# Attention pairs that take values, keys and queries in another order, with the value products moved into the score tiles

## The chip, the cores and the metric

The kernel runs on one core of one Trainium2 chip. The metric is the device time of one execution in microseconds (us); of several runs the median counts. A profile is one execution recorded by the hardware profiler. TensorE multiplies and transposes into PSUM; VectorE, ScalarE and GpSimd (DVE, ACT and POOL in the profile) work on what lies there and in SBUF; SyncE (SP) issues the transfers.

## What is computed

The reference is a block of two layers over 1024 latent and 256 context tokens of width 1024. Each layer norms its input, projects it, runs three mixers side by side (a gated linear recurrence with 4 heads, an mLSTM with 4 heads, and windowed attention with 6 heads of 64), gates their outputs, projects them back and adds the normed result to the input. The change lies in the attention:

```
def row_fn(r):                       # one of 16 rows of 64 latent tokens
    s_w = q_r . k(8 rows around r) + bias        # 16 columns around each query, else -inf
    s_c = q_r . k(context)                       # 256 keys, no bias
    p = softmax(concat(s_w, s_c))
    return p_w @ v(8 rows) + p_c @ v(context)
```

In layer 0 the 256 context tokens attend to one another too, without bias. In layer 1 only the latent tokens have outputs.

## The kernel before

All projections read the normed input, transposed, as a high and a low half, so each product is three matmuls (`mm`, line 311, through `cm_group`, line 344; transposes go through `tr`, line 317). A projection unit is one generator that yields after every three matmuls of one k of eight: a group of 512 tokens gives 8 yields; with the 256 context tokens a unit has 8 + 8 + 8 yields (the first 8 half as long), without them 16. `c0` to `c2` are the keys of the three head pairs (`natten_k`, line 1047), `d0` to `d2` the queries (`natten_q`, line 1074), `e0` to `e2` the values (`natten_v`, line 1059), `G0` to `G7` gates of the mixers' outputs (`gate_unit`, line 405; G2 to G4 have two projections). `W` loads the output weights (`out_weights`, line 1244: 32 loads, each rounded by ScalarE at line 1264 and subtracted by GpSimd at line 1265, into the buffers of the normed input), and `o0` to `o9` are tiles of the output projection (`out_tile`, line 1310; matmuls named u).

The order of TensorE's work is written by a planner, `drive` (line 455). It runs one generator, `mixers` (line 1413), whose own matmuls (recurrences, attention) go first; each number that this yields is a time in the planner's clock (`clk`, which every matmul advances by its columns / 2400, half of that for small ones) that is to be filled. It is filled by steps of units from `ORDER` (line 44), one unit at a time and each to its end; the next one is the first in the list whose conditions in `NEED` (line 53) are met. Yielding a name runs units until that one is done. If nothing can run, the clock is set forward and TensorE simply waits for its next operand. The waits are in `WAIT` (line 54). The other engines are put in order by a scheduler that sees the whole program; `ahead` gives instructions a priority.

After the two pairs of recurrence heads (`hgrn_head`, line 898; VectorE runs its state chain at line 989, the last products into op are at line 1011) the condition `o1` is set, the second recurrence norm follows (`hgrn_norm`, line 1016), and the attention pairs 0, 1 and 2 come. Before each, `mixers` asks for `c`, `d` and `e` of the pair, then transposes and splits the values (`natten_vt`, line 1094). `natten_pair` (line 1116) works in blocks of 128 queries and two heads: 2 + 8 blocks in layer 0, 8 in layer 1. A block has these parts:

- `scores` (line 1136): one PSUM tile of two banks (pool pb, two buffers, tiles sc) per head. Window scores end at column 512, the 256 context scores follow. The bias tile (tag RB, two buffers) gets the window bias by DMA and zeros for the context by a GpSimd memset (line 1143). VectorE adds both and takes the row's minimum (line 1156), ScalarE takes the exponential (1158) and divides (1160).
- `context` and `window` (lines 1169 and 1177): the probabilities are transposed in tiles tc and tw of pool pm (two buffers) and split by ScalarE and VectorE (lines 1166 and 1167) into Pc and Pw.
- `values` (line 1186): products of 10 matmuls in a tile pv of pool pm, emptied by ScalarE (1198) and VectorE (1199 and twice 1215).

The blocks are staggered, and the waits lie between:

```
b.context(); b.window(0); yield WAIT["t"]     # 0.3
nxt.scores()
b.window(1); yield WAIT["pt"]                 # 1.2
b.values();  yield WAIT["sc"]                 # 1.2, 3.0 after the first scores
```

So each block takes four buffers of pool pm in turn: tc, tw, tw, pv. Buffers `wt(i, ...)` are shared slots of SBUF. The values of a pair lie in slots 10 and 3, in which the blocks keep their split probabilities (Pw in 10 and 9, Pc in 3); the keys lie in slots (4, 5) and (0, 8) by turns; the queries of all pairs in 6 and 7. Therefore `e1` and `e2` wait for the end of the pair before (`n0`, `n1`), `d1` and `d2` for its last scores (`s0`, `s1`), while `c1` and `c2` can fill the blocks of the pair before.

Of the kernel before, what the change touches and what calls it, by code (L numbers as in the profile page):

```python
# [21 lines left out]
KD = 8  # L22
# [21 lines left out]
ORDER = ("p0 p1 v q0 p2 f0 f1 p3 q1 f2 f3 G0 G1 c0 G2 d0 e0 G3 c1 G4 d1 e1 c2 G5 d2 e2 G6 G7 W",) * 2  # L44
# [8 lines left out]
NEED = {"p2": ("b0",), "p3": ("b1",), "c0": ("A0",), "d0": ("o1",), "e0": ("A1",), "c1": ("o1",), "G4": ("o1",), "d1": ("s0",), "e1": ("n0",), "c2": ("s0",), "d2": ("s1",), "e2": ("n1",), "W": ("c2", "d2", "e2", "G7", "gg")} | {f"o{t}": ("W",) for t in range(10)}  # L53
# [10 lines left out]
def _build(ctx, tc, nc, I, out, dbg, upto):  # L64
# [40 lines left out]
    XS = ((3, 4, 5, 6, 8, 1, 11, 7, 9, 3), (1, 2, 3, 9, 11, 12, 6, 7, 4, 5))  # L105
# [10 lines left out]
    V.memset(mhalf, -0.5)  # L116

# [929 lines left out]
    def natten_k(l, p, hx):  # L1047

        kh, kl = [wt(((4, 5), (0, 8))[p % 2][i], [P, TA], f"ck{l}_{p}_{i}", F32R) for i in range(2)]
# [9 lines left out]
    def natten_v(l, p, hx):  # L1059

        cv = S["cv", p] = [wt((10, 3)[i], [P, TC + 8 * CWID], f"cv{l}_{p}_{i}") for i in range(2)]
# [12 lines left out]
    def natten_q(l, p, hx):  # L1074
# [4 lines left out]
        def evq(t0, N, ps):  # L1079
# [9 lines left out]
            V.tensor_tensor(view(qs[1]), src, hi.bitcast(F32), op=ALU.subtract)  # L1089

        yield from proj_cm(hx, I["wcm"][l, 6 + 3 * p + 0], LATG if l == 1 else ALLG, evq, f"Cq{l}_{p}")
        S["q", p] = qs

    def natten_vt(l, p):
# [4 lines left out]
        for i, cbs in ((0, None), (0, (0, 3)), (0, (1, 2)), (1, (0, 3)), (1, (1, 2))):  # L1099
# [10 lines left out]
            for m in range(0, len(o), n):  # L1110
# [3 lines left out]
                V.tensor_tensor(lo, v, hi.bitcast(F32), op=ALU.subtract)  # L1114

    def natten_pair(l, p):
# [4 lines left out]
        if p == 2:  # L1121
            S["yC"] = wt(0, [P, TA], f"yC{l}")
# [3 lines left out]
        class Block:  # L1126
# [9 lines left out]
            def scores(self):  # L1136

                nm, nk, rb, cb = self.nm, self.nk, self.rb, self.cb
                self.S2, bias, ps = [], [], []
# [420 lines left out]
```

## Time and profile before

| | |
|---|---|
| median of three runs | 2108.16 us (2107.46 to 2115.57) |
| profiled execution | 2102.49 us, of it 2100.7 us span from first to last instruction |
| TensorE matmuls busy | 1816.6 us, 86% |
| VectorE / ScalarE / GpSimd busy | 1338.9 / 885.5 / 727.8 us |
| mean granted TensorE clock | 0.931 |
| transfers | 199.32 MB, a mean of 95 GB/s |

Times in rows are us from the first instruction. The attention of layer 0 lies between about 700 and 1080, that of layer 1 between about 1720 and 2025. In a timeline each row is a start, a length, the engine and line, the operation, what it writes and reads, and a count where equal neighbours are merged; in square brackets stands the idle time of the engine before it and what ended it. PEclk is the clock that TensorE was granted, as a share of 2.4 GHz; the lower level, 1.2 GHz, is 0.5.

### The profile page before, as it was taken

What the parts mean: (1) busy time and instruction counts of PE and PEld (TensorE: products, weight loads), DVE (VectorE), ACT (ScalarE), POOL (GpSimd) and SP (SyncE); (2) the same over time, 40 slices, a digit from 0 to 9 for tenths busy, and PEclk for the clock granted to TensorE, in tenths of its full rate; (3) what the DMA queues carried; (4) which work ended last, traced back from release to release, by engine and by line L of the source; (5) the groups of instructions that cost most, each with busy time, mean ns of one, the idle gap of its engine ahead of it and who ended that gap; (6) DMA issues with size and microseconds to landing.
All of it is one profiled execution on the core that took longest, in us unless ns stands there. A gap on an engine that the chain in (4) does not pass through costs nothing.

```text
span 2100.7 us, 34868 instructions
## 1 busy us (share of the span) xinstructions
PE 1816.6 (86%) x12842; PEld 1559.3 (74%) x12842; DVE 1338.9 (64%) x3117; ACT 885.5 (42%) x2029; POOL 727.8 (35%) x746
## 2 busy tenths in 40 slices
PE   6988889988878888987799988999979798988798
PEld 3977888877666776766678888989767677767577
DVE  7697777778498458353565586464786954443564
ACT  5433433453232256364553434353532325554641
POOL 5342342254371112024124444234454621201512
PEclk8989999998889999978899999999999999997799
DMA  7122333530311222134354112132404011213443
GB/s 301 61 80 74 106 111 108 171 108 26 114 39 44 91 83 96 34 99 143 99 190 142 35 45 84 50 124 97 147 32 131 26 53 50 87 35 94 141 137 106
DMA packets 143723, 199.32 MB, mean 95 GB/s; under 512 B 13128, under 2 KB 89960, under 8 KB 143552
## 3 DMA queue, kind: packets, MB, share of 16 engines
q1 hardware_dynamic: 143552, 197.09, 29.1%
q8 instruction: 101, 1.65, 0.3%
q14 instruction: 70, 0.57, 0.1%
HBM read 154.35 MB, written 42.70 MB: 94 GB/s over the span
## 4 chain that ended last, share of the span: by engine, by line
PE 45%; DVE 27%; issue 8%; ACT 8%; DMA 5%; POOL 4%; DVEq 0%; POOLq 0%; ACTq 0%; SPq 0%
PE u L315 8%; PE ppB L315 7%; DVE F L945 6%; PE ppCv L315 4%; PE ppCq L315 4%; PE ppAf L315 3%; DVE dj L199 3%; PE ppGz L315 3%; DVE S L989 2%; PE ppAq L315 2%; ACT S L1158 2%; PE ov L315 2%; PE ppAv L315 2%; ACT S L1160 2%; DVE AT L926 2%
## 5 line engine op out<-in xcount | busy, mean ns | idle before, releaser
L315 PE MATMUL ppB<-whB,hh 128*128 128x288 f32 (+3 forms) x640 | 198.2, 310 | 23.9 <-ACT Vx L606 18.3
L315 PE MATMUL ppB<-whB,hl 128*128 128x288 f32 (+3 forms) x640 | 193.2, 302 | 1.0 <-DVE hl L293 1.0
L315 PE MATMUL ppB<-wlB,hh 128*128 128x288 f32 (+3 forms) x640 | 193.1, 302 | 0.0
L315 PE MATMUL u<-ow,yh 128*128 128x512 f32 (+1 forms) x684 | 185.3, 365 | 0.3 <-ACT u L1386 0.3
L945 POOL TENSOR_TENSOR F<-F,FG 64x640 f32<-64x640 f32 x72 | 142.1, 1974 | 74.5 <-DVE FG L946 58.4
L945 DVE TENSOR_TENSOR F<-F,FG 64x640 f32<-64x640 f32 (+1 forms) x120 | 150.5, 1256 | 3.0
L199 DVE CUSTOM_DVE_ANT_0 dj<-wm,crows 128x256 bf16<-128x256 f32 x256 | 129.7, 507 | 32.3 <-DMA wm<-in_w_mod 28.9
L315 PE MATMUL ppGz<-hh,whGz 128*128 128x512 f32 (+1 forms) x320 | 132.5, 414 | 20.4 <-DVE gz L422 13.3
L315 PEld LDWEIGHTS ppB<-whB,hh 128*128 128x128 f32 x640 | 125.4, 196 | 26.8 <-ACT Vx L606 20.2
L315 PEld LDWEIGHTS u<-ow,yh 128*128 128x128 f32 x684 | 122.2, 191 | 19.2 <-ACT u L1386 0.5
L1143 POOL MEMSET bias<- 128x256 f32 x96 | 29.7, 312 | 297.5 <-DVE nmx L1156 283.4
L315 PEld LDWEIGHTS ppB<-whB,hl 128*128 128x128 f32 x640 | 125.0, 195 | 1.3 <-DVE hl L293 1.3
L315 PEld LDWEIGHTS ppB<-wlB,hh 128*128 128x128 f32 x640 | 125.3, 196 | 0.1
L315 PE MATMUL ppGz<-hh,wlGz 128*128 128x512 f32 (+1 forms) x320 | 123.8, 387 | 0.6 <-POOL wlGz L325 0.6
L315 PE MATMUL ppGz<-hl,whGz 128*128 128x512 f32 (+1 forms) x320 | 124.2, 388 | 0.0
L932 ACT ACTIVATE ZK<-F,half 128x640 f32<-128x640 f32 (+1 forms) x96 | 70.6, 786 | 106.0 <-POOL F L945 77.7
L315 PE MATMUL u<-ow,yl 128*128 128x512 f32 (+1 forms) x324 | 114.7, 372 | 0.0
L315 PE MATMUL gr<-F,ZK 128*64 128x64 f32 x1728 | 70.3, 245 | 48.4 <-DVE F L945 34.6
L315 PEld LDWEIGHTS gr<-F,ZK 128*64 128x64 f32 x1728 | 64.6, 158 | 59.3 <-issue 37.0
L315 PEld LDWEIGHTS ppGz<-hh,whGz 128*128 128x128 f32 x320 | 64.5, 201 | 34.8 <-DVE gz L422 15.3
L989 DVE SCALAR_TENSOR_TENSOR S<-S,dec,up 64x64 f32<-64x64 f32 x288 | 80.5, 280 | 9.2
L1158 ACT ACTIVATE S<-S,nmx 128x544 f32<-128x544 f32 (+1 forms) x96 | 75.1, 783 | 24.2 <-DVE nmx L1156 22.8
(443 smaller groups left out, 5327.8 us busy)
## 6 DMA issues: line engine op xcount, KB each, us to landing
wm<-in_w_mod SPq DMA_DIRECT2D x64, 256.0 KB
bias<-in_rpb SPq DMA_DIRECT2D x48, 192.0 KB
ygr<-gTd SPq DMA_DIRECT2D x36, 256.0 KB
wm<-in_w_first SPq DMA_DIRECT2D x16, 512.0 KB
wrGz<-in_wcm SPq DMA_DIRECT2D x32, 256.0 KB
gTd<-gz SPq DMA_DIRECT2D x32, 256.0 KB
wro<-in_w_out SPq DMA_DIRECT2D x32, 256.0 KB
wrB<-in_wB SPq DMA_DIRECT2D x24, 288.0 KB
```

The lines of the kernel that those rows point to most:

```text
L199: V.tensor_tensor_reduce(out=junk, in0=w, in1=r, scale=1.0, scalar=0.0, op0=ALU.mult, op1=ALU.add, accum_out=dst[:, i:i + 1])
L315: return PE.matmul(out, lhsT=lhsT, rhs=rhs, start=start, stop=stop)
L926: V.copy_predicated(AT[:, y0:, :], lmask[:, None, li, :].to_broadcast([P, NT - y0, LA]), src)
L932: A.activation(vw(ZK)[:, tok0 // (2 * m):, s_, :], vw(T1)[:, tok0 // (2 * m):, s_, :], AF.Copy, scale=half[:, s_:s_ + 1])
L945: eng.tensor_tensor(x, x, d[r, n0:].to_broadcast([64, nb - n0, m]), op=ALU.mult)
L989: V.scalar_tensor_tensor(Sx[r, nx, :], Sx[r, c, :], dec[r, c:c + 1], ups[c][r], op0=ALU.mult, op1=ALU.add)
L1143: G.memset(bias[i][:, nk:nk + TC], 0.0)
L1158: A.activation(S2, S2, AF.Exp, scale=-1.0, bias=nmx[:, o], accum_out=den[:, o])
L1160: A.activation(S2, S2, AF.Copy, scale=den[:, o])
```

## The change

The order in each pair becomes values, their transposes, keys, blocks. Values lie in slots 4 and 5; `e1` and `e2` need only the value transposes of the pair before (new conditions `vt0` and `vt1`); the keys always lie in 0 and 8 and wait for the last scores of the pair before, as do the queries. The first values (`e0`) take the place of the first keys among the units that run under the second pair of recurrence heads; `c0` waits for `o1`. `G7` waits for `s1`. A block waits for its own group of queries alone (context, first or second 512 tokens). The value products of a block go into columns 768 to 1023 of the two score tiles of the next block, in the bank of its context scores; only a pair's last block still takes a tile of pool pm. Their emptying is split by head. The context part of the bias comes as zeros with the bias DMA; blocks of context queries add a constant zero. Slots of the result of pair 2, of the low half in `out_prep` and of the next layer's input move with these.

```
-ORDER = ("... f3 G0 G1 c0 G2 d0 e0 G3 c1 G4 d1 e1 c2 G5 d2 e2 G6 G7 W",) * 2
+ORDER = ("... f3 G0 G1 e0 G2 c0 d0 G3 e1 G4 c1 d1 e2 G5 c2 d2 G6 G7 W",) * 2
...
-NEED = {..., "c0": ("A0",), "d0": ("o1",), "e0": ("A1",), "c1": ("o1",), "G4": ("o1",), "d1": ("s0",), "e1": ("n0",), "c2": ("s0",), "d2": ("s1",), "e2": ("n1",), "W": ("c2", "d2", "e2", "G7", "gg")}
+NEED = {..., "e0": ("A0",), "c0": ("o1",), "d0": ("o1",), "G4": ("o1",), "e1": ("vt0",), "c1": ("s0",), "d1": ("s0",), "e2": ("vt1",), "c2": ("s1",), "d2": ("s1",), "G7": ("s1",), "W": ("c2", "d2", "e2", "G7", "gg")}
...
-    XS = (..., (1, 2, 3, 9, 11, 12, 6, 7, 4, 5))
+    XS = (..., (0, 1, 2, 3, 9, 11, 12, 6, 7, 8))
...
+    zero = cst.tile([P, 1], F32, name="zero")
+    V.memset(zero, 0.0)
...
     def natten_k(l, p, hx):
-        kh, kl = [wt(((4, 5), (0, 8))[p % 2][i], [P, TA], f"ck{l}_{p}_{i}", F32R) for i in range(2)]
+        kh, kl = [wt((0, 8)[i], [P, TA], f"ck{l}_{p}_{i}", F32R) for i in range(2)]
...
     def natten_v(l, p, hx):
-        cv = S["cv", p] = [wt((10, 3)[i], [P, TC + 8 * CWID], f"cv{l}_{p}_{i}") for i in range(2)]
+        cv = S["cv", p] = [wt((4, 5)[i], [P, TC + 8 * CWID], f"cv{l}_{p}_{i}") for i in range(2)]
...
     def natten_q(l, p, hx):
...
             V.tensor_tensor(view(qs[1]), src, hi.bitcast(F32), op=ALU.subtract)
+            done.add(f"d{p}_{(t0 - TC) // 512 if t0 else None}")
+
+        S["q", p] = qs
         yield from proj_cm(hx, I["wcm"][l, 6 + 3 * p + 0], LATG if l == 1 else ALLG, evq, f"Cq{l}_{p}")
-        S["q", p] = qs
...
     def natten_vt(l, p):
...
+        done.add(f"vt{p}")
...
     def natten_pair(l, p):
...
-            S["yC"] = wt(0, [P, TA], f"yC{l}")
+            S["yC"] = wt(4, [P, TA], f"yC{l}")
...
             def scores(self):
...
-                    bias.append(sm.tile([P, NWIN + TC], F32, tag="RB", name=f"bias{nm}_{i}"))
-                    G.memset(bias[i][:, nk:nk + TC], 0.0)
+                    bias.append(sm.tile([P, NWIN + TC], F32, tag="RB", name=f"bias{nm}_{i}") if nk else None)
                     if nk:
-                        nc.sync.dma_start(bias[i][:, 0:nk], I["rpb"][l, 2 * p + i, 3 * rb + (0, 1, 1, 2)[cb], :, 0:nk])
+                        nc.sync.dma_start(bias[i][:, 0:nk + TC], I["rpb"][l, 2 * p + i, 3 * rb + (0, 1, 1, 2)[cb], :, 0:nk + TC])
...
-                    V.tensor_tensor_reduce(out=S2, in0=ps[i][:, 512 - nk:512 + TC], in1=bias[i][:, :nk + TC],
+                    V.tensor_tensor_reduce(out=S2, in0=ps[i][:, 512 - nk:512 + TC], in1=bias[i][:, :nk + TC] if nk else zero.to_broadcast([P, TC]),
...
-            def values(self):
+            def values(self, nxt):
...
-                pv = pm.tile([P, 512], F32, tag="pm", name="pv" + self.nm)
+                if nxt:
+                    pvs = [ps[:, 768:1024] for ps in nxt.ps]
+                else:
+                    pv = pm.tile([P, 512], F32, tag="pm", name="pv" + self.nm)
+                    pvs = [pv[:, 0:256], pv[:, 256:512]]
...
-                A.activation(o, pv[64:128, :, 0], AF.Copy)
-                V.tensor_tensor(o, o, pv[0:64, :, 1], op=ALU.add)
+                for i in range(2):
+                    A.activation(o[:, i], pvs[i][64:128, 0:P], AF.Copy)
+                    V.tensor_tensor(o[:, i], o[:, i], pvs[i][0:64, P:2 * P], op=ALU.add)
...
             if nxt:
+                yield f"d{p}_{nxt.rb}"
                 nxt.scores()
...
-                b.values()
+                b.values(nxt)
...
     def out_prep(l, t):
-        yl = ... else wt(8, [P, KD, P], f"yl{l}_{t}", F32R)
+        yl = ... else wt(5, [P, KD, P], f"yl{l}_{t}", F32R)
...
         def mixers():
             for p in range(3):
-                yield f"c{p}"
+                yield f"e{p}"
                 if p == 0:
                     yield from hgrn_norm(l, 1)
-                yield f"d{p}"
-                yield f"e{p}"
                 yield from natten_vt(l, p)
+                yield f"c{p}"
```

The table of biases that the host lays out gets 256 more columns, of zeros.

## Rows read from the trace of the kernel before

**Rows 1.** Windows: length, busy time and records by engine, granted clock, DMA share, GB/s.

```profile
741.00:834.00 93.00, 79.53 (x492) 64.73 (x491) 65.92 (x227) 59.31 (x136) 18.89 (x30) 0.94 0.30 96
926.00:945.00 19.00, 13.34 (x68) 10.06 (x67) 9.33 (x25) 12.38 (x25) 5.83 (x7) 0.63 0.51 158
978.00:1008.00 30.00, 12.15 (x59) 8.44 (x58) 14.43 (x34) 15.77 (x40) 23.64 (x27) 0.57 0.66 210
1745.00:1818.00 73.00, 63.17 (x418) 50.90 (x417) 41.22 (x106) 49.47 (x101) 16.01 (x25) 1.00 0.25 78
1882.00:1914.00 32.00, 22.48 (x119) 16.40 (x119) 16.89 (x43) 19.17 (x39) 6.77 (x10) 0.68 0.35 106
1945.00:1973.00 28.00, 14.72 (x72) 11.43 (x71) 14.39 (x31) 18.99 (x41) 23.52 (x26) 0.55 0.65 210
```

**Rows 2.** Timeline of one block with filler, layer 1, pair 0.

```profile
1783.82 1.02 PE L315 MATMUL sc<-ck,cq 64*128 64x256 f32 x12
...
1785.63 0.72 DVE L1156 CUSTOM_DVE_ANT_0 S<-sc,bias 128x544 f32<-128x544 f32 x1
...
1787.28 1.38 ACT L1160 ACTIVATE S<-S,den 128x544 f32<-128x544 f32 x2
...
1787.72 0.40 PE L315 MATMUL ppGo<-hh,whGo 128*128 128x512 f32 x1
...
1789.11 0.60 PE L320 MATMUL tc<-ident,S 128*128 128x128 f32 x4
...
1790.26 0.50 PE L320 MATMUL tw<-ident,S 128*96 128x128 f32 x3 [0.55 <-DVE yTC L1215]
...
1791.40 1.15 PE L315 MATMUL sc<-ck,cq 64*128 64x256 f32 x12
```

**Rows 3.** Waits of TensorE, 735 to 1080: us in total, times, longest.

```profile
PE tw L320 <- DVE yTC L1215: 4.2, 5, 1.1
PE tw L320 <- DVE yC L1215: 3.9, 3, 2.0
...
PE vtp_(1, 2)_8536 L320 <- DVE VT L1114: 1.5, 1, 1.5
```

**Rows 4.** The same waits, 1740 to 2026.

```profile
PE tw L320 <- DVE yTC L1215: 11.9, 11, 1.7
...
PE tw L320 <- DVE yC L1215: 3.2, 4, 1.1
```

**Rows 5.** Timeline of the opening of pair 2, layer 0.

```profile
988.82 9.49 POOL L1265 TENSOR_TENSOR ow<-wro,ow 128x512 fp32r<-128x512 f32 x10
...
998.26 0.55 POOL L1143 MEMSET bias_None<- 128x256 f32 x2
...
1002.80 0.42 DVE L1156 CUSTOM_DVE_ANT_0 S_None<-sc_None,bias_None 128x256 f32<-128x256 f32 x1
```

**Rows 6.** Timeline of TensorE, layer 1, end of pair 1: first and fourth scores.

```profile
1884.95 1.01 PE L315 MATMUL sc<-ck,cq 64*128 64x256 f32 x12
...
1911.76 1.73 PE L315 MATMUL sc<-ck,cq 64*128 64x256 f32 x12
```

**Rows 7.** Tile cq: evictions of queries, ns minimum, median, maximum.

```profile
L1088 ACT ACTIVATE cq<-ppCq x15: 367/597/600, 711.1 to 1930.9; 128x512 fp32r<-128x512 f32 x12, 128x256 fp32r<-128x256 f32 x3
```

**Rows 8.** Windows, tile ppGz alone (gate projections); the first count is TensorE's matmuls.

```profile
864.00:927.00 63.00, 18.70 (x72) 12.82 (x72) 1.11 (x2) 1.90 (x4) 0.95 0.19 56
1655.00:1719.00 64.00, 38.69 (x144) 27.63 (x144) 4.06 (x6) 7.00 (x12) 0.95 0.14 46
```

**Rows 9.** Timeline, end of the recurrence in layer 1.

```profile
1709.91 4.96 DVE L989 SCALAR_TENSOR_TENSOR S<-S,dec,up 64x64 f32<-64x64 f32 x16
...
1717.08 2.09 PE L315 MATMUL op<-S,F 128*64 128x64 f32 x64
```

**Rows 10.** DMA issues of the bias.

```profile
bias<-in_rpb SPq DMA_DIRECT2D x48, 192.0 KB
...
bias<-in_rpb SPq DMA_DIRECT2D x48, 144.0 KB
```

More of the change, by code (lines that the diff above doesn't have):

```diff
@@ L43 @@
 MT = 36
-ORDER = ("p0 p1 v q0 p2 f0 f1 p3 q1 f2 f3 G0 G1 c0 G2 d0 e0 G3 c1 G4 d1 e1 c2 G5 d2 e2 G6 G7 W",) * 2
+ORDER = ("p0 p1 v q0 p2 f0 f1 p3 q1 f2 f3 G0 G1 e0 G2 c0 d0 G3 e1 G4 c1 d1 e2 G5 c2 d2 G6 G7 W",) * 2
 ORDER = ORDER[0] + "".join(f" o{t}" for t in range(10)), ORDER[1] + "".join(f" o{t}" for t in range(2, 10))
@@ L52 @@
 EV = 3500
-NEED = {"p2": ("b0",), "p3": ("b1",), "c0": ("A0",), "d0": ("o1",), "e0": ("A1",), "c1": ("o1",), "G4": ("o1",), "d1": ("s0",), "e1": ("n0",), "c2": ("s0",), "d2": ("s1",), "e2": ("n1",), "W": ("c2", "d2", "e2", "G7", "gg")} | {f"o{t}": ("W",) for t in range(10)}
+NEED = {"p2": ("b0",), "p3": ("b1",), "e0": ("A0",), "c0": ("o1",), "d0": ("o1",), "G4": ("o1",), "e1": ("vt0",), "c1": ("s0",), "d1": ("s0",), "e2": ("vt1",), "c2": ("s1",), "d2": ("s1",), "G7": ("s1",), "W": ("c2", "d2", "e2", "G7", "gg")} | {f"o{t}": ("W",) for t in range(10)}
 WAIT = {"gate": 28.0, "rot": 14.0, "qkT": 0.8, "ov": 1.4, "yB": 9.0, "load": 8.0, "gr": 4.0, "ktp": 1.5, "up": 8.0, "upc": 3.0, "yA": 9.0, "vtp": 0.5, "sc": 1.2, "sc0": 3.0, "t": 0.3, "pt": 1.2, "W": 8.0, "prep": 8.0, "st": 6.0, "y": 2.0}
@@ L103, in x_src @@
         return x1d[t * P:(t + 1) * P]
-    XS = ((3, 4, 5, 6, 8, 1, 11, 7, 9, 3), (1, 2, 3, 9, 11, 12, 6, 7, 4, 5))
+    XS = ((3, 4, 5, 6, 8, 1, 11, 7, 9, 3), (0, 1, 2, 3, 9, 11, 12, 6, 7, 8))
     ssx = cst.tile([P, NT], F32, name="ssx")
@@ L1138, in scores @@
                 nm, nk, rb, cb = self.nm, self.nk, self.rb, self.cb
-                self.S2, bias, ps = [], [], []
+                self.S2, bias, self.ps = [], [], []
+                ps = self.ps
                 for i in range(2):
                     self.S2.append(wk.tile([P, 5 * P], F32, tag=f"h{i}", name=f"S2{nm}_{i}"))
-                    bias.append(sm.tile([P, NWIN + TC], F32, tag="RB", name=f"bias{nm}_{i}"))
-                    G.memset(bias[i][:, nk:nk + TC], 0.0)
+                    bias.append(sm.tile([P, NWIN + TC], F32, tag="RB", name=f"bias{nm}_{i}") if nk else None)
                     if nk:
-                        nc.sync.dma_start(bias[i][:, 0:nk], I["rpb"][l, 2 * p + i, 3 * rb + (0, 1, 1, 2)[cb], :, 0:nk])
+                        nc.sync.dma_start(bias[i][:, 0:nk + TC], I["rpb"][l, 2 * p + i, 3 * rb + (0, 1, 1, 2)[cb], :, 0:nk + TC])
                     ps.append(pb.tile([P, 1024], F32, tag="pb", name=f"sc{nm}_{i}"))
@@ L1193, in values @@
                     for m, (r, pt, vt) in enumerate(tiles):
-                        mm(pv[:, i * 2 * P:(i + 1) * 2 * P], vt[0:r, i].rearrange("p i d -> p (i d)"),
+                        mm(pvs[i], vt[0:r, i].rearrange("p i d -> p (i d)"),
                            pt[0:r].rearrange("p i q -> p (i q)"), m == 0, m == n - 1)
-                pv = pv.rearrange("p (h i q) -> p h i q", h=2, i=2)
                 o = sm.tile([64, 2, P], F32, tag="On", name="o" + self.nm, bufs=1)
-                A.activation(o, pv[64:128, :, 0], AF.Copy)
-                V.tensor_tensor(o, o, pv[0:64, :, 1], op=ALU.add)
+                for i in range(2):
+                    A.activation(o[:, i], pvs[i][64:128, 0:P], AF.Copy)
+                    V.tensor_tensor(o[:, i], o[:, i], pvs[i][0:64, P:2 * P], op=ALU.add)
                 if p == 2:
@@ L1209, in values @@
                 for i, hs in enumerate(HS):
-                    v = [o[:, i], pv[0:64, i, 0]]
+                    v = [o[:, i], pvs[i][0:64, 0:P]]
                     if rb is None:
@@ L1286, in out_prep @@
         yh = hxp.tile([P, KD, P], F32R, tag=("hl6", "hh7")[t % 2], name=f"yh{l}_{t}")
-        yl = hxp.tile([P, KD, P], F32R, tag="hl7", name=f"yl{l}_{t}") if t % 2 else wt(8, [P, KD, P], f"yl{l}_{t}", F32R)
+        yl = hxp.tile([P, KD, P], F32R, tag="hl7", name=f"yl{l}_{t}") if t % 2 else wt(5, [P, KD, P], f"yl{l}_{t}", F32R)
         for s in range(2):
@@ L1512, in layout @@
     rpb = f("na_rpb")
-    rp = np.concatenate([rpb.reshape(2, HC, -1), np.full((2, HC, 1), NEG, np.float32)], axis=2)
-    idx = np.full((6, P, NWIN), 15 * 31, np.int64)
+    rp = np.concatenate([rpb.reshape(2, HC, -1), np.full((2, HC, 1), NEG, np.float32), np.zeros((2, HC, 1), np.float32)], axis=2)
+    idx = np.full((6, P, NWIN + TC), 15 * 31 + 1, np.int64)
     for rb in range(2):
```

## The prediction

> **What bounds the kernel now.** I read the windows by stage first. TensorE is the engine that is nearly always at work, so what can be won is the time in which it stands still or runs at its lower clock. In the attention stretches that time is large: of the 93 us of the first pair of layer 0 it works 79.5, of the 73 us of the first pair of layer 1 63.2. Four short stretches are worse: 926 to 945, 978 to 1008, 1882 to 1914 and 1945 to 1973, with a granted clock of 0.55 to 0.68 [rows 1]. A clock of 0.57 between the levels 2.4 and 1.2 GHz is 86% of the time at the lower one, so of 12.15 us of work some 5.2 are excess; with 17.9 us idle, 978 to 1008 loses 23 us. The same working gives 20 us for 1945 to 1973, 17 for 1882 to 1914 and 11 for 926 to 945.
>
> Then I read one block in order of time, and the waits that last longest. A block with filler work takes 7.6 us from scores to scores (1783.82 to 1791.40). The chain of the softmax is not late in it: its scaling ends at 1788.66 and the transposes of the probabilities start at 1789.11. What is late is the second transpose tile: 0.55 us of idle, ended by the last addition that empties the value products, since the small PSUM pool has two buffers [rows 2]. Over both layers this wait sums to 4.2 + 3.9 + 11.9 + 3.2 = 23 us [rows 3, 4].
>
> Last I looked at why 978 to 1008 is so bad. No filler is left there, and the output weights are being split: GpSimd runs ten subtractions from 988.82 to 998.31, and only then the two memsets of the bias tile, without which the score reduction, here at 1002.80, cannot start [rows 5].
>
> **Filler, counted in steps.** A step is what the planner inserts at once: three matmuls of 512 columns, 0.70 us (two steps from 1787.72 to 1789.11 [rows 2]). The planner's waits (0.3, 1.2, 1.2 against its own 0.64 a step) ask for 5 steps a block, and 5 before the second block. Ten blocks of layer 0 take 46 steps up to the last scores, eight of layer 1 take 36. A projection is 20 steps with context, 16 without. A block without filler takes 8.94 us (three from 1884.95 to 1911.76 [rows 6]), against 7.6 - 3.5 = 4.1 for its own part of a filled one: 4.8 us lost for 5 missing steps, about 1 us a step.
>
> **Part by part.**
>
> *a. Value products in the next block's score tiles.* The pool's second tile no longer waits for them; the 23 us can go. Late next is either the softmax (0.45 us of slack in the block shown) or the next scores, which now wait until the value products have left their tile. Those left it at about 1790.2, and the next scores came at 1791.40; 0.55 us earlier still leaves about half a microsecond [rows 2]. Emptying is split by head: one more ScalarE and one more VectorE instruction in each of 54 blocks, beside other work. I take 17 of the 23; bounds 0 and 23.
>
> *b. Opening of the third pair.* Now its queries and values run unmixed before it and nothing is left. After, the values of pair 2 are filler of pair 1, the keys run from the last scores of pair 1 on, and the second half of the queries and gate unit 7 (held until then) are filler: 35 steps in layer 0, 7 + 16 = 23 in layer 1. The bias memset leaves GpSimd's queue. The loss of 23 + 20 = 43 us goes. Bounds 0 and 43.
>
> *c. Output weights in the middle of the third pair.* Their unit needs gate unit 7, so it now comes when the filler ends, after about 6 of 10 and 3.6 of 8 blocks; the planner holds the output tiles 8 us more. A bare block is about 5.6 us to the planner (2.7 of waits and the rest its matmuls), so 1.4 blocks stay bare: 1.4 x 5 = 7 us a layer. The splits also cross the blocks' softmax on ScalarE, and the loads the bias transfers on SP's queue: 3 us a layer, an estimate between 0 and the loss of the old opening, taken low because the memset is gone. Together +20; bounds +8 and +57.
>
> *d. Starts of blocks.* A block that begins with its own queries waits for their eviction: one ScalarE pass of 0.60 us [rows 7] and a VectorE pass like it, less the one step of the next group that lies between: about 1.2 us, six times, +7. The value transposes in front of pair 2 keep the 1.8 us that they cost before the other pairs, of which 1.5 is one wait [rows 3], +4. Together +11; bounds +4 and +14.
>
> *e. End of the second pair.* Filler there was the keys of pair 2, and in layer 0 gate unit 7 as well (72 matmuls in 864 to 927 [rows 8]): 40 and 20 steps. After it is 15 + 20 = 35 and 7 + 20 = 27. Missing before the last scores (with one step used by the transposes before): 7 and 17 steps, after: 11 and 9. At 1 us a step +4 and -8: -4. Bounds -10 and +6. In pair 0 there is more than enough in both kernels; what remains of gate unit 4 runs unmixed, at nothing.
>
> *f. Tail of the recurrence, layer 1.* There gate units 5, 6 and 7 ran under the second pair of heads (144 matmuls from 1655 to 1719 [rows 8]). Without unit 7, 16 steps or 11.2 us of cover are missing. The stage can then end only when VectorE's state chain does, at 1714.87, and its last products take 2.09 us: 1717 instead of 1719.2 [rows 9]. 11.2 - 2.7 (one gate eviction on VectorE leaves too) = +8; bounds 0 and +11.
>
> *g. Costed at nothing.* 96 memsets of 0.3 us leave GpSimd, which is idle in most of these stretches [rows 1]. The bias transfers of 192 and 144 KB [rows 10] grow by 128 KB each, 12.6 MB in all. Two take 256 KB more a block, 1.2 us at the 210 GB/s of 978 to 1008 [rows 1], and are asked for when the last reduction ends, a block ahead. That cover would go only where loads stand in front of them (c). Values instead of keys under the recurrence are as many matmuls. The other buffer numbers only make (b) possible.
>
> Sum: -17 - 43 + 20 + 11 - 4 + 8 = **-25 us**. The profiled execution took 2102.49 us, so 2077.5. The median of the runs shown, 2108.16, lies 5.7 us above it; against that I forecast 2083.
>
> **The rivals.** *Bank.* The value products lie in the 512 columns that hold the context scores too, and may have to wait until VectorE has read both heads there. In the filled block that reading ends at 1786.35 (1785.63 + 0.72), and the products began at about 1786.5 [rows 2], so nothing is lost; in a bare block, two steps short, about 1 us is, in some 2.2 + 1.8 + 1.4 + 1.4 = 7 bare blocks: 2090. The Trainium skill, PSUM — Partial Sum Buffer, section "PSUM bank collisions raise a hardware error", states the rule, to guard PSUM by bank and not by address; no row of this kernel shows two engines' work of this kind in one bank. Against the price: in bare blocks the products already waited for their own probabilities.
>
> *The wait moves (no change).* If the next scores wait for the emptied tile as long as the second transposes did, (a) is 0: -8, 2100. For it: ScalarE empties late, behind the scaling; against it: about 1 us more of TensorE's work lies between.
>
> *The weights hold the blocks (slower).* In the middle of pair 2 the splits and the loads may cost what they cost at its opening, 43 us over both layers, on top of the 14 of bare blocks: -25 - 20 + 57 = +12, 2120. It decides if the bias of the next block comes behind more than about 15 us of weight loads, or scaling behind as many splits. For it: 978 to 1008 and 1945 to 1973 move 210 GB/s, a DMA share of 0.65 [rows 1]. Against it: part of that loss was the memset and the missing filler.
>
> *More than forecast.* All 23 in (a), the low bounds of (c) and of the starts: -23 - 43 + 8 + 6 - 4 + 8 = -48, 2060. That the change does not do what it says would show in (b): if gate unit 7 or the queries are not there as filler, only (a) and the losses remain, near no change; I count it with that case.
>
> **How the numbers follow.** Forecast 0.42 (2083), more 0.18 (2060), bank 0.10 (2090), no change 0.20 (2100), slower 0.10 (2120). A measurement can tell about 0.5%, 10.5 us, from no change, so the first three are faster: 0.70; same 0.20; slower 0.10. The range holds all but the slow case and the end of the fast one, with the bounds of (c) and (e): 2055 to 2112.
>
> **What would show it.** Right: no wait of the second transposes for the added outputs; matmuls of the query projection and of gate unit 7 between the blocks of pair 2, and a clock near 1 there; a lower clock and 7 to 11 us of idle at the recurrence's end in layer 1; about one and a half bare blocks after the last gate matmul. Wrong: scores that wait for the emptied value products, reductions that wait for the bias transfer, or the splits of the weights in front of the softmax in pair 2.

## The result, and the profile after

The changed kernel takes 2077.07 us (median, 2075.42 to 2078.59), the kernel before, beside it, 2107.81: a ratio of 0.9849 [0.982, 0.9878], 31 us faster where 25 were forecast. The profiled execution took 2076.41 us. The forecast of 2083 is 6 us off. Its parts did not all come out as written, and this section looks at each place that they named.

The page after: TensorE's share, and what the transfers moved.

```profile
PE 1817.6 (88%) x12842; PEld 1560.7 (75%) x12842; DVE 1340.1 (65%) x3172; ACT 885.7 (43%) x2083; POOL 696.4 (34%) x638
DMA packets 143434, 210.85 MB, mean 102 GB/s; under 512 B 13096, under 2 KB 77640, under 8 KB 143264
```

TensorE is busy as long as before, to the microsecond (1817.6 against 1816.6), at the same mean granted clock (0.932 against 0.931), so the gain is time in which it stood still. Four stretches of its timeline, cut at the same matmuls in both kernels, say where:

| stretch of TensorE's timeline, us | before | after |
|---|---|---|
| start to the last op of layer 0 | 692.0 | 697.6 |
| from there to layer 1's first gate transposes (attention, output tiles, first projections) | 517.6 | 494.3 |
| from there to the last op of layer 1 (recurrences) | 509.6 | 506.1 |
| from there to the last output product | 374.6 | 369.4 |

The first stretch is older work that the change hardly touches, and differs by 5.6 us between these two executions; that is why they lie 26 us apart and the medians 31. The attention of layer 0 gives 23 us, layer 1 with the tail of its recurrence 9. The terms of the forecast, taken by layer (the products by their waits, the weights and the starts in halves), said about 10 and 16.

First the block. Timeline of a filled block after, layer 1, pair 0, to be laid beside [rows 2]:

```profile
1748.69 1.01 PE L317 MATMUL sc<-ck,cq 64*128 64x256 f32 x12
...
1750.39 0.72 DVE L1160 CUSTOM_DVE_ANT_0 S<-sc,bias 128x544 f32<-128x544 f32 x1
...
1751.42 0.39 PE L317 MATMUL sc<-Pc,VT 128*128 128x256 f32 x2
...
1754.00 0.60 PE L322 MATMUL tc<-ident,S 128*128 128x128 f32 x4
...
1754.44 0.49 PE L322 MATMUL tw<-ident,S 128*96 128x128 f32 x3
...
1755.56 1.01 PE L317 MATMUL sc<-ck,cq 64*128 64x256 f32 x12
```

It takes 6.87 us from scores to scores instead of 7.6, with five filler steps in it as before. The second transposes (tw) come at once; the products (sc<-Pc) go into the next tile, right after VectorE has read both heads there (1750.39 + 0.72 = 1751.11).

Waits of TensorE after, first the longest, the fourth and the shortest of 740 to 1036, then the two longest of 1720 to 1987: us in total, times, longest.

```profile
PE tc L322 <- ACT S L1164: 13.1, 16, 1.6
...
PE sc L317 <- DVE nmx L1160: 3.9, 8, 1.0
...
PE sc_None L317 <- DVE cq L1091: 0.2, 1, 0.2
...
PE tc L322 <- ACT S L1164: 10.4, 14, 1.8
PE sc L317 <- DVE nmx L1160: 6.6, 2, 6.4
```

The waits for yTC and yC, 23 us in [rows 3, 4], are gone. Late next is the scaling of the softmax (tc<-ACT S), with 13.1 and 10.4 us no more than before (11.6 + 8.3 and 10.8, the 11.6 for blocks of context queries). No scores wait for emptied products in either window, so the wait did not move there. Products that wait for the score reduction in their bank (sc<-DVE nmx) are the rival "bank": 3.9 us in eight waits, and 6.6 us in two, of which one is 6.4 and has another cause (below).

Now the stretches that lost most in [rows 1]. Windows after: the opening of pair 2 in layer 0 and in layer 1, then where the output weights are split in each, the end of pair 1 in layer 1, and the tail of its recurrence.

```profile
947.30:977.30 30.00, 29.48 (x192) 24.05 (x192) 17.89 (x57) 20.12 (x49) 0.00 (x0) 1.00 0.36 112
1909.40:1936.00 26.60, 25.87 (x169) 20.92 (x168) 15.90 (x45) 20.09 (x46) 3.72 (x4) 1.00 0.44 142
985.00:1015.00 30.00, 18.82 (x90) 13.84 (x92) 17.76 (x40) 23.58 (x55) 25.77 (x26) 0.70 0.75 242
1936.00:1966.00 30.00, 16.45 (x80) 12.12 (x79) 16.62 (x39) 21.67 (x49) 22.44 (x23) 0.67 0.81 258
1856.00:1889.00 33.00, 26.64 (x158) 21.47 (x157) 17.87 (x49) 21.77 (x49) 7.62 (x6) 0.79 0.39 121
1656.40:1698.00 41.60, 26.91 (x281) 21.89 (x279) 28.63 (x88) 8.02 (x15) 5.32 (x8) 0.82 0.14 51
```

The openings are full: 0.5 and 0.7 us idle, clock 1.00. The hole has moved with the weights. By the working of the prediction (idle, and half the work that ran at the lower level) 985 to 1015 loses 11.2 + 18.82 x 0.6 x 0.5 = 17 us and 1936 to 1966 loses 13.6 + 16.45 x 0.66 x 0.5 = 19. Both openings had lost 43; these two lose 36.

What happens in such a stretch, in layer 1's timeline after:

```profile
1937.27 1.76 ACT L1274 ACTIVATE ow<-wro 128x512 fp32r<-128x512 f32 x4
...
1939.74 0.76 DVE L1304 TENSOR_TENSOR ygr<-ygr,yr 128x512 f32<-128x512 f32 x1 [2.39 <-DMA ygr<-gTd]
...
1942.70 0.88 PE L322 MATMUL tw<-ident,S 128*96 128x128 f32 x3 [2.87 <-DVE Pc L1171]
...
1950.18 1.83 SPq L427 DMA_DIRECT2D gTd<-gz  x1
...
1952.35 1.97 PE L317 MATMUL sc<-ck,cq 64*128 64x256 f32 x12
...
1955.94 0.63 ACT L1274 ACTIVATE ow<-wro 128x512 fp32r<-128x512 f32 x1 [3.52 <-DMA wro<-in_w_out]
...
1956.89 1.56 DVE L1304 TENSOR_TENSOR ygr<-ygr,yr 128x512 f32<-128x512 f32 x1 [3.75 <-DMA gTd<-gz]
...
1961.55 0.77 PE L317 MATMUL sc<-Pc,VT 128*128 128x256 f32 x2 [6.42 <-DVE nmx L1160]
...
1966.65 1.97 PE L317 MATMUL sc<-ck,cq 64*128 64x256 f32 x12
```

ScalarE's queue holds the splits (ow<-wro) between the parts of the softmax, and in front of some of them it stands for the load of the weights: 3.5 us before 1955.94, and 3.4 and 4.2 us in all in pair 2 of the two layers. VectorE's holds the preparation of output tiles (ygr): before 1939.74 it stood 2.4 us for a load, and before 1956.89 3.75 us, by the profile for the store of gate unit 7's own output, issued at 1950.18. Behind the first stands the split of Pc that tw waits for, behind the second the score reduction that the products wait for. The two blocks with splits take 13.5 and 14.3 us (1938.82, 1952.35, 1966.65), against 8.94 for a bare block in [rows 6].

### The profile page after: what moved, and what is told of

It is laid out like the page before. It is cut to its first block, busy times and chain, and to the rows that moved or that the text cites. A ratio compares the mean times of both kernels' runs of the same rounds, so it can differ in the third digit from the quotient of the medians.

```text
span 2074.5 us, 34916 instructions
## 1 busy us (share of the span) xinstructions
PE 1817.6 (88%) x12842; PEld 1560.7 (75%) x12842; DVE 1340.1 (65%) x3172; ACT 885.7 (43%) x2083; POOL 696.4 (34%) x638
## 2 busy tenths in 40 slices
DMA packets 143434, 210.85 MB, mean 102 GB/s; under 512 B 13096, under 2 KB 77640, under 8 KB 143264
## 4 chain that ended last, share of the span: by engine, by line
PE 46%; DVE 27%; issue 10%; ACT 6%; DMA 5%; POOL 3%; SPq 0%; DVEq 0%; POOLq 0%; ACTq 0%
PE u L317 8%; PE ppB L317 7%; DVE F L947 6%; PE ppGz L317 4%; PE ppAf L317 4%; PE ppCk L317 4%; DVE dj L201 3%; DVE S L991 3%; PE ppCq L317 2%; PE ppAv L317 2%; PE ppAq L317 2%; PE sc L317 2%; PE ov L317 2%; DVE AT L928 2%; DVE FG L948 2%
## 5 line engine op out<-in xcount | busy, mean ns | idle before, releaser
L317 PE MATMUL ppGz<-hh,whGz 128*128 128x512 f32 (+1 forms) x320 | 132.2, 413 | 13.8 <-DVE gz L424 10.0
L1275 POOL TENSOR_TENSOR ow<-wro,ow 128x256 fp32r<-128x256 f32 (+1 forms) x44 | 43.7, 1026 | 122.3 <-ACT ow L1274 122.3
```

What stands on the lines that cost most here:

```text
L317: return PE.matmul(out, lhsT=lhsT, rhs=rhs, start=start, stop=stop)
L1275: G.tensor_tensor(w, raw[:, c:c + n], h.bitcast(F32), op=ALU.subtract)
```

## The experiments

Times are medians, each with the median of the kernel before in the same set of runs; the stretches are the last three of the table above, of the profiled execution. "Change" is the changed kernel.

| kernel | us | before beside it | ratio, 95% interval | stretches, us |
|---|---|---|---|---|
| change | 2077.07 | 2107.81 | 0.9849 [0.982, 0.9878] | 494.3 / 506.1 / 369.4 |
| e1 before + products | 2088.38 | 2111.55 | 0.9896 [0.9866, 0.9927] | 507.7 / 516.4 / 359.3 |
| e2 before + zeros by DMA | 2112.21 | 2111.55 | 1.0001 [0.9983, 1.0019] | 513.0 / 518.0 / 376.1 |
| e3 order alone, emptying by head | 2136.48 | 2111.55 | 1.0126 [1.0098, 1.0154] | 523.6 / 510.4 / 391.3 |
| e4 change, filler moved later | 2051.01 | 2111.55 | 0.9722 [0.9697, 0.9748] | 486.4 / 499.9 / 364.7 |
| e5 change with memset | 2069.5 | 2108.44 | 0.9806 [0.9782, 0.9831] | 491.1 / 508.2 / 367.1 |
| e6 change without products, emptying by head | 2130.63 | 2108.44 | 1.0094 [1.0067, 1.0121] | 521.5 / 515.2 / 390.9 |
| e7 change, unit 7 not held | 2060.53 | 2108.44 | 0.9768 [0.9741, 0.9795] | 490.9 / 510.3 / 355.6 |
| e8 change, whole queries first | 2104.88 | 2108.44 | 0.9972 [0.9958, 0.9986] | 519.7 / 504.3 / 374.8 |
| e9 gates spread, unit 7 early | 2038.25 | 2112.14 | 0.9651 [0.9636, 0.9665] | 484.7 / 504.0 / 349.6 |
| e10 e9 with memset | 2038.88 | 2112.14 | 0.9651 [0.9636, 0.9665] | 484.1 / 504.1 / 351.1 |
| e11 weights after pair 2 | 2088.01 | 2113.2 | 0.9882 [0.9849, 0.9916] | 497.3 / 508.6 / 374.4 |
| e12 splits wholly on GpSimd | 2062.11 | 2113.2 | 0.9756 [0.9725, 0.9787] | 488.0 / 508.3 / 362.2 |

The middle stretch holds the recurrences, which the edits touch at most in their filler, and it lies anywhere between 500 and 518 us; so a difference of a few us in one stretch of one execution decides nothing.

**e1: the value products alone,** in the kernel before.

```
-                b.values()
+                b.values(nxt)          # and the body of values() as in the change
```

> The kernel before with one part of the change: the value products in the next block's score tiles, emptied by head; order, slots and bias as before. Theory (the 23 us of second transposes waiting for the emptied products go, and most of it is kept): 17 to 20 us less than before, about 2089, no wait of tw for an added output in the trace, filled blocks of 7.0 instead of 7.6 us from scores to scores. Rival (the wait only moves to the next scores or to the softmax): within 4 us of before, 2104 to 2108, with as much idle time before sc or tc as tw has lost.

23 us faster (0.9896, so 15 to 28), a little over its theory: the whole sum of the waits in [rows 3, 4]. The stretches of the two attentions are 10 and 15 us shorter, where these waits sum to 8.1 and 15.1.

**e2: the zeros alone.** Memsets out, bias by the longer transfer, in the kernel before.

```
-                    G.memset(bias[i][:, nk:nk + TC], 0.0)
-                        nc.sync.dma_start(bias[i][:, 0:nk], ...)
+                        nc.sync.dma_start(bias[i][:, 0:nk + TC], ...)
```

> The kernel before with one part of the change: zeros of the bias by DMA, none for blocks of context queries. Theory (memsets matter only where GpSimd splits the output weights in front of them): at the opening of pair 2 in layer 0 the 8.7 us of idle before the second context block shrink to 2 or 3, some 3 us in layer 1, nothing elsewhere: 2098 to 2101. Rival (the opening is short of filler, so another wait takes the place): 2105 to 2108.

Nothing in the median, as the rival said. The opening of pair 2 in layer 0 shows why. The reduction in [rows 5] is that of the second block of context queries; the first block's came at 989.51, in front of the memsets. And behind the memsets, which ended at 998.81, the second stood another 4 us behind VectorE's additions for an output tile. In the kernel before:

```profile
989.51 0.42 DVE L1156 CUSTOM_DVE_ANT_0 S_None<-sc_None,bias_None 128x256 f32<-128x256 f32 x1 [1.22 <-PE sc_None L315]
...
998.75 1.70 DVE L1294 TENSOR_TENSOR ygr<-ygr,yr 128x384 f32<-128x384 f32 x1 [3.85 <-POOL bias_None L1143]
```

In e2 the second reduction comes early, but the same addition then stands 3.4 us for GpSimd, whose ten subtractions lie in front of what it waits for, and the softmax behind it:

```profile
1000.35 0.41 DVE L1157 CUSTOM_DVE_ANT_0 S_None<-sc_None,zero 128x256 f32<-128x256 f32 x1
...
1005.07 0.56 DVE L1295 TENSOR_TENSOR ygr<-ygr,yr 128x384 f32<-128x384 f32 x1 [3.40 <-POOL yl L1298]
...
1006.64 0.69 PE L322 MATMUL tc_None<-ident,S_None 128*128 128x128 f32 x2 [3.54 <-ACT S_None L1161]
```

The second block takes 8.3 us instead of 12.4, and the stretch of layer 0 is 4.6 us shorter in this execution, less than can be told from one; the medians show none of it.

**e3: the order alone.** The change, with products in tiles of pool pm and the memset. The emptying by head stays.

```
-                b.values(nxt)
+                b.values(None)         # and bias as in the kernel before
```

> The changed kernel with the value products back in a tile of the small pool and the zeros back by memset: order, slots, conditions and starts by query group stay. Theory (order is worth -43 + 14 + 6 + 11 - 4 + 8 = -8, and the memsets now stand behind the weight splits in the middle of pair 2, +5): 2099 to 2106. Rival (the order is the whole gain): 2077 to 2082. In the trace the openings of pair 2 have filler, the tail of the recurrence of layer 1 idles some 11 us.

Both expectations missed: 25 us slower than before. TensorE's longest wait in layer 0 (690 to 1080):

```profile
PE tw L322 <- DVE Pc L1172: 23.7, 13, 4.6
```

In the kernel before it was 2.9 us, in four waits.

**e6: the change without the products alone** (the first edit of e3, zeros by DMA kept; the emptying by head stays here too).

> The changed kernel with the value products back in a tile of the small pool (emptying by head stays); zeros by DMA and the order stay. Theory M (zeros carry the joint gain, the products only their own 23): 2097 to 2105. Rival P (the products carry it): 2120 to 2137, near the order alone.

54 us slower than the change, as rival P said: in the new order, leaving them out costs more than twice what they bring alone. Waits in layer 0 (734 to 1061) and rows of the timeline at the longest of them:

```profile
PE tw L322 <- DVE Pc L1171: 23.1, 12, 4.4
PE pv L317 <- DVE Pw L1171: 13.5, 10, 2.8
```

```profile
1024.15 0.62 ACT L1274 ACTIVATE ow<-wro 128x512 fp32r<-128x512 f32 x1
...
1025.89 0.59 ACT L1170 ACTIVATE Pc<-tc 128x512 fp32r<-128x512 f32 x1
...
1027.34 0.88 PE L322 MATMUL tw<-ident,S 128*96 128x128 f32 x3 [4.40 <-DVE Pc L1171]
```

The probabilities' eviction, transposed by 1022.94 (1021.78 + 1.16), waits on ScalarE behind splits, output tiles and gates; meanwhile TensorE has no buffer for tw. That is one place. The price is 0.9 us a block on average of the 54 (some 49 of the 54 us lie in the first and last stretch), and no pair is free of it: from its first to its last scores e6 takes 6.0, 8.2 and 13.8 us longer than the change in layer 0, 7.0, 5.9 and 7.0 in layer 1. Part of it may not be the order at all. Emptying by head, a part of the change that was not undone here, occupies a buffer of the small pool for longer: from its first instruction on ScalarE to its last addition it takes 1.98 us (median of the 54 blocks) in e3 and e6, against 1.43 in the kernel before, where it went in one piece. No run has the new order with products in pool pm emptied in one piece, so the 25 us of e3 and the 54 of e6 hold what the emptying costs, and how much that is stays open.

**e8: whole queries before the blocks.**

```
-                yield f"d{p}_{nxt.rb}"
+                yield f"d{p}"
```

> The changed kernel, but blocks begin only when all queries of the pair are done (two groups in layer 1, three in layer 0, instead of one). Theory (queries under the first blocks are filler: pairs 1 and 2 lose 15 steps in layer 0 and 7 in layer 1 each, 44 steps; some come back as pair 0 leaves less of gate unit 4, the output weights come sooner): 15 to 40 us more than the changed kernel, 2092 to 2117. Rival (starting early only costs the wait for the eviction of the first group): 2070 to 2077.

28 us slower, as the theory said, 25 of it in layer 0. Windows of the query products alone (tile ppCq), of layer 1: in the changed kernel from the first values' transposes of pair 2 in layer 1 to its first scores and then its blocks, and the first of the two in e8.

```profile
1889.60:1909.40 19.80, 6.38 (x27) 5.09 (x27) 0.00 (x0) 0.60 (x1) 1.00 0.24 79
1909.40:1985.60 76.20, 5.67 (x22) 3.72 (x21) 1.39 (x2) 0.58 (x1) 0.84 0.52 166
```

```profile
1917.10:1942.50 25.40, 11.35 (x48) 9.04 (x48) 0.69 (x1) 1.18 (x2) 1.00 0.23 83
```

Nearly half of the 48 matmuls are filler in the change; in e8 all 48 run before the first scores. In layer 0, which lost most, it is 45 of the 72 in each pair against none, and the first scores of pair 0 come 48.3 us after the last op of the recurrence instead of 36.6.

**e7: gate unit 7 not held** until the last scores of pair 1.

```
-NEED = {..., "G7": ("s1",), ...}
+NEED = {...}
```

> The changed kernel without the condition of gate unit 7: it runs under the recurrence in layer 1 again, and in layer 0 as filler of pair 1. Account: in layer 1 the tail of the recurrence has its cover again (-8), pair 2 lacks 16 steps but the output weights come 16 steps sooner, and their output tiles then fill; in layer 0 pair 1 gains 11 steps (-11), pair 2 loses 20 (+20 less what output tiles fill). If a step in pair 2 is worth 1 us as in pair 1: 2080 to 2095. Rival (what matters in pair 2 is when the weights come, and holding unit 7 gains nothing): 2062 to 2074.

17 us faster than the change, below both expectations and on the rival's side, 14 of it in the last stretch: the hold cost time. Windows of pair 2, layer 1: the output products alone (tile u) in the kernel before, in the change and in e7; and in the change the gates alone (ppGz).

```profile
1944.80:2025.00 80.20, 25.08 (x103) 17.15 (x104) 2.04 (x3) 2.10 (x6) 0.83 0.43 133
```

```profile
1889.60:1985.60 96.00, 10.52 (x44) 7.61 (x45) 0.00 (x0) 0.00 (x0) 0.88 0.46 148
1889.60:1985.60 96.00, 14.55 (x48) 9.20 (x48) 1.38 (x2) 2.33 (x4) 0.88 0.46 148
```

```profile
1885.90:1982.90 97.00, 23.51 (x95) 15.97 (x96) 2.05 (x3) 2.08 (x6) 0.89 0.47 148
1655.90:1697.50 41.60, 36.47 (x315) 29.15 (x315) 25.77 (x87) 11.39 (x21) 5.73 (x8) 0.92 0.14 48
```

Unit 7 filled no hole in pair 2 of layer 1. Its 14.55 us took the place of some 13 us of output products, which then ran unmixed behind the attention (81.8 us from its last product to the end, 70.2 in e7), while the pair takes 96 us either way. What it left behind is the hole in the recurrence's tail: in e7 (the last row) the 41.6 us up to the last op hold 36.5 us of work at clock 0.92, in the change 26.9 at 0.82. That closing it saves time by itself is not shown: the stretch that holds it is 4 us longer in e7, within its spread.

**e4: filler moved later.** Gate unit 4 (two projections) may run under the recurrence; units 5 and 6, which ran there, are kept for the attention.

```
-ORDER = ("... G3 e1 G4 c1 d1 e2 G5 c2 d2 G6 G7 W",) * 2
+ORDER = ("... G3 G4 e1 G5 c1 d1 e2 G6 c2 d2 G7 W",) * 2
-NEED = {..., "G4": ("o1",), ...}
+NEED = {..., "G5": ("o1",), "G6": ("s0",), ...}
```

> The changed kernel with the gate units handed out otherwise: unit 4 (as long as 5 and 6 together) runs under the recurrence, unit 5 waits for o1 and fills pair 0, unit 6 waits for the last scores of pair 0 and fills pair 1; unit 7 as in the change. Nothing long is left unmixed after pair 0. Theory (a missing step costs 1 us; pair 1 misses 11 steps in layer 0 and 9 in layer 1): 15 to 20 us less than the changed kernel, about 2060, and no bare block in pair 1. Rival (bare blocks are bound by their own softmax chain and the filler then only adds TensorE work elsewhere saved at full speed): within 4 us of the changed kernel, 2073 to 2081.

26 us faster than the change, more than the theory's 15 to 20, with as many steps in all. By the profiled execution 8 and 5 us lie in the two stretches with attention. Another 6 lie up to the last op of layer 0 (691.7) and 6 in the middle stretch, and both of these differ as much between executions of other kernels, so that the edit saves anything there is not shown. One place is pair 1 of layer 1, here its window in the change and then in e4:

```profile
1787.80:1889.60 101.80, 92.76 (x550) 76.22 (x549) 45.96 (x123) 53.42 (x118) 15.94 (x12) 0.93 0.26 84
```

```profile
1769.80:1859.30 89.50, 83.53 (x516) 68.46 (x515) 44.01 (x121) 52.41 (x118) 10.12 (x9) 0.98 0.28 90
```

9.0 us idle and a clock of 0.93 become 6.0 and 0.98.

**e9: both,** unit 7 early and two others kept for pairs 1 and 2; **e10:** the same with the memset.

```
+ORDER = ("... G3 G4 G7 e1 c1 d1 e2 G5 c2 d2 G6 W",) * 2
+NEED = {..., "G5": ("o1",), "G6": ("s0",), ...}       # no G4, no G7; W waits for G5 and G6 too
```

> The changed kernel with the gate units handed out again: units 4 and 7 without condition (under the recurrence; in layer 0 unit 7 falls to pair 0), unit 5 waits for o1 and fills pair 0 of layer 1 and pair 1 of layer 0, unit 6 waits for the last scores of pair 0 and fills pair 1 of layer 1 and pair 2 of layer 0. Theory (the gain of units spread over the pairs, -26 over the change, and that of a covered tail of the recurrence with earlier output weights in layer 1, -12 of the -17, are of different places and add): 2036 to 2044. Rival (both are the same missing steps of pair 2): 2049 to 2056.

> As the run before, with the zeros of the bias by GpSimd's memset again and the smaller transfers. Theory (the zeros by DMA cost 12.6 MB of transfers and no memset stands on a path any more: 7 us better without, as in the change itself): 2029 to 2038, below the run before by 4 to 9. Rival (the 7 us were a difference of two sets of runs): within 3 us of the run before.

2038.25 us, 74 below the kernel before and 39 below the change, as the theory of e9 said: the gains of e4 (26) and e7 (17) nearly add. e10 is the same within 1 us, as its rival said.

**e5: the change with the memset back.**

> The changed kernel with the zeros of the bias back on GpSimd (memset, smaller transfer); products in the score tiles and the order stay. So far: products alone -23, zeros alone 0, order alone +25, all three -34, so 36 us come from parts working together. Theory M (with the weights split in the middle of pair 2, the memsets wait behind the splits on GpSimd; the zeros by DMA are worth little alone and much with the order): 2090 to 2105, and GpSimd's memsets late in front of the reductions of pair 2 in the trace. Rival P (it is the products: in the new order the two buffers of the small pool are the limit of every block, and zeros matter nowhere): 2074 to 2082.

8 us below the change, against both expectations; the intervals of the two ratios touch (0.9782 to 0.9831 and 0.982 to 0.9878). The pair e9 and e10, run on one chip in one set, does not show it, nor does e2; so I take the zeros to be worth nothing, and leave open what the 8 us are. The bias landed in 3.1 and 2.9 us with the zeros in it and in 2.5 and 2.3 without (medians from issue to landing).

**e11: weights after pair 2.**

```
-"W": ("c2", "d2", "e2", "G7", "gg")
+"W": ("c2", "d2", "e2", "G7", "gg", "n2")
```

> The changed kernel with one more condition on the unit of the output weights: it comes only after the last block of the third pair. Loads, splits and the preparation of the output tiles then lie behind the blocks, and no output tile can fill them. In the changed kernel the blocks in which the weights are split take 11.7 and 13.1 us from scores to scores in layer 0 (989.49, 1001.23, 1014.33) and 13.5 and 14.3 us in layer 1 (1938.82, 1952.35, 1966.65), with a granted clock of 0.70 and 0.67 in the two stretches of 30 us. Theory (the queues that the weights fill hold the softmax): without weights beside them the bare blocks of pair 2 take what a bare block took in the kernel before, about 9 us, and none takes over 10.5. Rival (they are slow because filler is missing and the clock is low): they stay at 11.5 to 14.5 us. Under both the kernel as a whole is slower than the changed one, since 22 us of GpSimd's subtractions a layer then stand in front of the output tiles: 2095 to 2140.

11 us slower than the change, less than both sides expected, and it says nothing on the question: only TensorE's order moved. The scheduler of the other engines let the splits run where they had run. Tile ow on ScalarE in e11 (ns minimum, median, maximum, first and last start; in the change the same row has 983.4 to 1955.9):

```profile
L1274 ACT ACTIVATE ow<-wro x44: 399/420/637, 983.5 to 1960.1; 128x256 fp32r<-128x256 f32 x24, 128x512 fp32r<-128x512 f32 x20
```

**e12: the splits' rounding on GpSimd.**

```
-                    A.activation(h, raw[:, c:c + n], AF.Copy)
+                    G.tensor_copy(out=h, in_=raw[:, c:c + n])
```

> The changed kernel with the rounding of the output weights taken from ScalarE to GpSimd, so that it stands no longer in the queue of the softmax; GpSimd, which does nothing else there, takes about twice as long over the weights. Theory A (the splits on ScalarE are what holds the blocks): the slow blocks of pair 2 (11.7, 13.1, 13.5 and 14.3 us) come down to 9 to 10.5, and the time falls by 5 to 12 us, to 2065 to 2072. Theory B (VectorE, standing behind the preparation of the output tiles, holds them): the two longest blocks stay at 13 us or more, and the time is 2075 to 2090, the weights being ready later.

15 us faster than the change by the medians (20 by the ratios), more than theory A asked. The blocks of pair 2 that took 11.7, 13.1, 13.5 and 14.3 us take 6.7, 8.4, 10.1 and 8.1. Windows of pair 2 in layer 0 and 1, then TensorE's two longest waits in that of layer 1; beside them the same windows of the change.

```profile
926.40:1023.60 97.20, 85.98 (x525) 69.67 (x524) 55.78 (x150) 55.67 (x130) 34.90 (x47) 0.95 0.50 165
1882.20:1971.00 88.80, 77.79 (x455) 61.64 (x454) 49.11 (x124) 49.38 (x108) 36.16 (x48) 0.94 0.51 160
```

```profile
PE tc L322 <- ACT S L1164: 3.4, 5, 1.9
PE sc L317 <- DVE nmx L1160: 3.0, 4, 1.0
```

```profile
930.00:1034.00 104.00, 89.25 (x525) 71.38 (x524) 56.24 (x150) 64.62 (x152) 27.24 (x27) 0.89 0.49 156
1889.60:1985.60 96.00, 79.49 (x455) 63.40 (x453) 48.88 (x124) 58.13 (x130) 26.16 (x26) 0.88 0.46 148
```

7 us a layer, as many matmuls, less idle time (11.2 and 11.0 instead of 14.8 and 16.5) and a clock of 0.95 and 0.94. The loads run no slower (165 and 160 GB/s against 156 and 148), so what held these blocks was what stood in the queues of the softmax, not the rate of the transfers. But e12 takes three things away at once. ScalarE is rid of the splits and of its waits for the loads in front of them (3.4 and 4.2 us; GpSimd now waits for loads, 2.2 and 4.4). And in layer 1 VectorE's work comes in another order: its waits for gate transfers fall from 7.0 to 0.6 us, and TensorE's wait of 6.4 us behind it has become one of 1.0. Which of the three is worth how much was not tried apart. Nor was e12's edit within e9.

## Why the prediction was right, and where its terms were not

The sign and the size held, and the likeliest case came about: the value products no longer hold the second transposes, and the opening of pair 2 is full. Of its signs of being wrong two did not appear: no scores wait for emptied products, and by the profile VectorE waits for no bias transfer in either attention. The third did, the splits in front of the softmax.

That the total fits to 6 us is in part luck. The prediction put the order and all that follows from it at -8, from windows of the kernel before. With the products already in, order and zeros are worth 11 us (from e1 to the change; the two intervals just overlap); in the kernel before, the order with its emptying by head costs 25 (e3). The prediction did not say which of the two its -8 meant. And inside it errors cancel: (c) is 16 too small, the hold of unit 7 counted as a gain, (d) too large, and 6.6 us were not seen at all. The terms:

*a, the products (-17).* Under-sized. Alone they give 23 (e1), the upper bound; in the new order, leaving them out costs 54 (e6). The prediction priced each part against the kernel before and added up. The parts interact: alone, products give -23, zeros 0 and the order +25, together +2, and the three in one kernel -31; of the difference of 33 a part not measured is the emptying by head, which e1 and e3 both pay. Its own bound, "0 and 23", came from waits in the old order, and need not hold in the new one.

*b, the opening (-43).* As written by the rows: both openings run at clock 1.00 with hardly any idle time. The memset, which the prediction listed among the causes, is worth nothing that e2 or e10 can tell. The prediction misread the row at 1002.80 in [rows 5]: between the memsets and this reduction VectorE still had the additions for an output tile, and with the memsets gone these stand behind GpSimd's subtractions themselves (e2).

*c, the weights in the middle (+20).* This is the term that failed by size: 36 by the same working, near the old loss of 43. "3 us a layer ... taken low because the memset is gone" is the step: taking the splits off ScalarE gives about 7 a layer back (e12). It is the rival "the weights hold the blocks" at about half its price, (b) having been won in full; "scaling behind splits" was its mechanism; the trace shows it, and e12 bears it out, though not apart from ScalarE's waits for the loads. The second cause, VectorE's queue behind output tiles and unit 7's store, no case had named.

*b and c, the filler.* "Gate unit 7 (held until then)" as filler of pair 2 was counted as a gain. In layer 1 it displaced output products of the same length (e7), and holding it was a loss of 17.

*d, starts (+11).* The blocks that begin with their own queries wait 0.2 us in layer 0 and not at all in layer 1, not 7: other groups' steps lie between. The longest wait of the value transposes before a pair is 1.6 to 2.0 us, near the 1.8 said. That starting so is worth 28 (e8) was not priced as such; only what it does for pair 2 lies within (b).

*e, the end of pair 1 (-4).* 1856 to 1889 loses 6.4 + 26.64 x 0.42 x 0.5 = 12, where 1882 to 1914 lost 17. The rule behind it, about 1 us for a missing step, holds in direction: e4 puts filler where it was missing and gains 26. What the end of pair 1 in layer 0 (+4) came to was not looked at apart.

*f, the tail (+8).* TensorE's idle time in the 41.6 us up to the last op went from 6.4 to 14.7 us: +8.3, and the clock fell from 0.96 to 0.82. The last product waited for VectorE's state chain, as said. The window before, and the product in the timeline after:

```profile
1677.60:1719.20 41.60, 35.23 (x318) 27.84 (x316) 27.78 (x89) 11.49 (x21) 6.05 (x9) 0.96 0.17 55
...
1695.98 1.98 PE L317 MATMUL op<-S,F 128*64 128x64 f32 x32 [8.53 <-DVE S L991]
```

*g (0).* The transfers grew to 210.85 MB from 199.32 and cost nothing that e2 or e10 could see.

*Not in the sum: gate weights.* In layer 0 of the kernel before TensorE waited 2.6 + 2.6 + 0.8 + 0.6 = 6.6 us for the rounded weights of gate units, in one block each of pairs 0 and 1 (759.85 to 772.60 and 887.35 to 900.12, 12.8 us each). In the change other filler comes first, the wait is gone, and the same blocks take 8.8 and 7.4 us; in e1, with the old order, it is still there.

*The fast case* took +6 for (d), whose low bound is +4; nothing hangs on it.

*Bank.* The products do wait for VectorE's reduction in their bank, up to 1.0 us at a time in layer 0 and 3.9 in all. The Trainium skill, PSUM — Partial Sum Buffer, section "PSUM bank collisions raise a hardware error", asks for such a guard by bank; this trace agrees that the program waits so, and prices it at about half a microsecond a time (3.9 us in eight waits). It is small beside the 23 that the move saves.

## What to carry to other kernels

Filler is worth what it fills: before holding work back for a hole, look at what would have run there without it, and what the work leaves behind where it was. When work is moved into the middle of a softmax, go through each engine's queue for what stands in front of which part of it, also for instructions that stand there for a transfer, and put the work on the engine whose queue nobody waits for (here its operands lay in SBUF). Parts that change the order and parts that change buffers can't be priced one by one against the old kernel: leave one part out of the whole, too, before believing its price, and see that all of that part is out.

## What the runs showed that was not expected

The rounding of the weights was no dearer on GpSimd: the records of e12 have a median of 403 ns for its 44 casts (24 of 128x256 elements, 20 of 128x512), those of the change 418 ns for the same on ScalarE (the profile's spans on GpSimd are rough). The Trainium skill, Perfetto Trace Analysis, section "Optimizing GPSIMD Operations", says to prefer other engines where possible; here the measurement decides against it, by 15 us, because the work left ScalarE's queue. Removing the 108 memsets of the bias from GpSimd (the prediction counted the 96 of window blocks) did nothing measurable (1.0001 [0.9983, 1.0019]), even where ten subtractions stood in front of two of them.
